# A list made later, three more up-products, and the first block of each group expert by expert

## The chip, the cores and the metric

The kernel runs on one core of a Trainium2 chip. The metric is device time in microseconds (us). The core has five engines that each run their own queue of instructions in order: TensorE (PE, with its weight loads shown apart as PEld), VectorE (DVE), ScalarE (ACT), GpSimd (POOL) and SyncE (SP, which here only issues DMA transfers). They wait for each other through semaphores.

## What is computed

The reference is one residual block of an encoder over 512 tokens of width 2048, in float32: a mixer (stick-breaking attention and forgetting attention, gated), then PEER, a retrieval of single-neuron experts, then a norm. The change touches PEER alone:

```python
q = (ht @ w_query).reshape(n_tok, 8, 2, 128)
scores = einsum('thpc,hpnc->thpn', q, sub_keys)
s1, i1 = top_k(scores[:, :, 0], 16); s2, i2 = top_k(scores[:, :, 1], 16)
cand_score = (s1[..., :, None] + s2[..., None, :]).reshape(n_tok, 8, 256)
cand_id = (i1[..., :, None] * 128 + i2[..., None, :]).reshape(n_tok, 8, 256)
top_score, pos = top_k(cand_score, 16)
expert_ids = take_along_axis(cand_id, pos); gates = softmax(top_score)
act = gelu(einsum('thkd,td->thk', expert_u[expert_ids], x))
out = einsum('thk,thkd->td', gates * act, expert_v[expert_ids])
```

So each token has 8 heads with 16 experts each, out of 16384.

## The kernel before, in words

The first 1300 us hold the mixer; then come the output projection, the second norm, and PEER. PEER treats its tokens in two ways.

**Dense tokens.** 352 tokens (`TD`) go through all experts. An "up-product" (`expert_up`, L532) makes the activations of 128 experts: it loads the weights in two halves (`wload`, L96), splits each into a high part `wh` (ACT, L108) and a low part `wl` (DVE, L109), and runs, per half, eight steps of three matmuls (L116 high by high, L117 high by low, L118 low by high), 48 matmuls in all into `psu`. There are 128 up-products. Raw weights `wr` have four buffers, `wh` and `wl` three each. Up-products made ahead (`early`, L618) store their result in device memory (`gact_sp`); `NS` of them, 54 before, are made that way: five behind each head's choice of experts for the dense tokens, and further ones between the gate tables.

The gates stand in 22 gate tables (L782 to L798), each for 16 tokens: PE products `psgt`, copied by ACT, sent to device memory (`gsp`) by POOL.

Then 16 groups of eight "weight tables" follow. `weigh(n)` (L813) takes the activations of 128 experts (`fetch`: loaded from `gact_sp`, L807, or made then by an up-product), for the first of a group loads the gates of the whole group into the one table buffer, which lies in the spare columns of h2 (three transfers on SP, L820, called `h<-gsp` in the profile), multiplies both on DVE (L822), and splits the result `wg` in high (ACT, L825) and low (DVE, L826). A group has eight blocks (`jb`), each with two outputs (`jj`), and each output sums over the group's eight expert tables `c`: 24 matmuls into `psy`. Behind an output, DVE adds it to `acc` (L846). The weights of output `jj` of a block are the `jj`-th half that its `wload` brings.

**Other tokens.** 128 tokens, and 32 more (the "second tile", `idx_b`, `gate_b`, `rstd_b`), take their experts' rows one by one: POOL gathers a row of 2048 numbers for each of 128 tokens (`row_of`, L554), DVE works on it for 2.35 us (L565, L574, L583, L594). These stand in a list `todo`; `pace` (L546) hands out a row behind splits of up-products and behind adds, at a rate that spreads them over the rest of the program. The list of the second tile (L746 to L763) is made by a product `psrep` of PE (L755) from DVE's `rep`, and copied out by DVE in four groups.

**What sets the order.** The code is written once; a layer below records the instructions and orders them with a list scheduler by its own costs, so an engine's queue isn't in the order of the code, but each engine runs its queue in order. `choose` (L650 to L711) is the choice of experts of one head, some 150 short DVE instructions.

Of the kernel before, what the change touches and what calls it, by code (L numbers as in the profile page):

```python
# [8 lines left out]
F32 = mybir.dt.float32  # L9
# [3 lines left out]
AF = mybir.ActivationFunctionType  # L13
ALU = mybir.AluOpType
# [4 lines left out]
P = 128  # L19
T = 512  # L20
NT = T // P
D = 2048
KC = D // P
HD = 128
NH = 8
NK = 128
TOPK = 16
HK = NH * TOPK
# [3 lines left out]
GC = 8  # L32
NG = NK // GC
JJ = D // (GC * P)
TB = 16
MB = 32
GB = P // MB
SB = HK // GB
TD = T - P - MB
# [1 line left out]
HT = NT - 2  # L41
CW = 112
UPS = 5
NS = NH * UPS + TD // TB - -(-(TD // TB) // 3)
SLOW = 0.8
LEAD = 1
NP = 4
# [3 lines left out]
def block_kernel(ctx, tc, xT, gains, w_vf, bf, w_qk, w_v, w_g, w_br, w_o, w_q, keysT, uT, vP, expert_u, expert_v, outT):  # L51
    nc = tc.nc
# [27 lines left out]
    ident = cp.tile([P, P], F32, name="ident")  # L80
    select(ident, zeros, 1, -1, ALU.not_equal, 1.0)
    g_sb = cp.tile([P, 3 * KC], F32, name="g_sb")
    nc.sync.dma_start(g_sb, gains)
    rstd = cp.tile([P, T], F32, name="rstd")
    rstd_t = cp.tile([P, NT], F32, name="rstd_t")
    one_c = ones[:, 0:1]

    acc = ap_.tile([P, KC, T], F32, name="acc")
# [6 lines left out]
    def wload(src, between=None, pace=None):  # L95

        out = []
        n = src.shape[-1] // 2
        for s in range(2):
            turn[0] += 1  # L100
            rp = more[0] if more and turn[0] % 2 else wp
            raw = rp.tile([P, WC], F32, tag="wr", name="wr", bufs=2)[:, :n]
            nc.sync.dma_start(raw, src[:, s * n:(s + 1) * n])
            if between and s == 0:
                between()
            hi = wp.tile([P, WC], F32R, tag="wh", bufs=3, name="wh")[:, :n]
            lo = wp.tile([P, WC], F32R, tag="wl", bufs=3, name="wl")[:, :n]
            nc.scalar.activation(hi, raw, AF.Copy)  # L108
            ins = nc.vector.tensor_tensor(lo, raw, hi.bitcast(F32), op=ALU.subtract)  # L109
            out.append((hi, lo))  # L110
            if pace:
                pace(ins, 0.5)
        return out

    def mm3(ps, wh, wl, ah, al, start, stop):
        nc.tensor.matmul(ps, wh, ah, start=start, stop=False)  # L116
        nc.tensor.matmul(ps, wh, al, start=False, stop=False)  # L117
        nc.tensor.matmul(ps, wl, ah, start=False, stop=stop)  # L118
# [19 lines left out]
    with ExitStack() as s1:  # L138
# [3 lines left out]
        with ExitStack() as s2:  # L142
# [21 lines left out]
            for k in range(KC):  # L164
# [3 lines left out]
                                               op1=ALU.subtract)  # L168
# [252 lines left out]
            ps = pa.tile([P, NT, NH], F32, tag="z1", name="psc")  # L421
# [5 lines left out]
            ps = pa.tile([P, T], F32, tag="z0", name="pscT")  # L427
# [34 lines left out]
        h2 = h2p.tile([P, KC, 2, T], F32R, name="h2")  # L462
        with ExitStack() as s2:
            op = pool("oproj", 1, cm=s2)
# [23 lines left out]
    gl = pool("gelu", 4)  # L488
# [129 lines left out]
    def early(n, pace=None):  # L618
        for _ in range(n):
            if len(started) < NS:  # L620
                c = len(started)
                nc.scalar.dma_start(gact_sp[c], expert_up(c, pace))
                started.append(c)

    with ExitStack() as s1:
# [88 lines left out]
        for h in range(NH):  # L714
            sc = []
            sv = se.tile([P, 2, HT, NK], F32, tag="sv", name="sv")
            for p in range(2):
                b = 2 * h + p
                if b == 1:
                    norm2()  # L720
                if b == 3:
                    token_rows(lambda k: acc[:, k, T - P:], h2g, accg)
                ps = pu.tile([P, T], F32, tag="pu", name="psq2")
                proj(ps, wload(w_q[b]), h2)
                q = se.tile([P, T], F32, tag="ab1", name="q2")
                nc.scalar.activation(q, ps, AF.Copy)
                kt = se.tile([P, NK], F32, tag="kt", name="kt")
                nc.sync.dma_start(kt, keysT[b])
                ps = psx.tile([P, NT, NK], F32, tag="psx", name="pss")
                for t in range(NT):  # L730
                    nc.tensor.matmul(ps[:, t], q[:, t * P:(t + 1) * P], kt, start=True, stop=True)
                nc.scalar.activation(sv[:, p], ps[:, :HT], AF.Copy)
                sc.append(ps[:, HT:])
            nc.scalar.dma_start(scores[h], sv)
            choose(h, sc, HT, NT - HT)


        for k in range(KC):
            tmp = gl.tile([P, TD], F32, tag="gl", name="h2n")
            nc.vector.scalar_tensor_tensor(tmp, acc[:, k, :TD], g_sb[:, KC + k:KC + k + 1], rstd[:, :TD], op0=ALU.mult,  # L740
                                           op1=ALU.mult)
            nc.scalar.activation(h2[:, k, 0, :TD], tmp, AF.Copy)
            nc.vector.tensor_tensor(h2[:, k, 1, :TD], tmp, h2[:, k, 0, :TD].bitcast(F32), op=ALU.subtract)


        nc.vector.scalar_tensor_tensor(idx, ia[:, NT - 1], float(NK), ib[:, NT - 1], op0=ALU.mult, op1=ALU.add)  # L746
        nc.vector.tensor_copy(ggate, gt[:, NT - 1])
        rep = se.tile([P, 2 * HK + 2], F32, tag="ab1", name="rep")
        nc.vector.scalar_tensor_tensor(rep[:, :HK], ia[:, NT - 2], float(NK), ib[:, NT - 2], op0=ALU.mult, op1=ALU.add)
        nc.vector.tensor_copy(rep[:, HK:2 * HK], gt[:, NT - 2])  # L750
        nc.vector.tensor_copy(rep[:, 2 * HK:], rstd_t[:, NT - 2:NT - 1].to_broadcast([P, 2]))
        spread = se.tile([P, GB, MB], F32, tag="kt", name="spread")
        nc.vector.tensor_copy(spread, ident[:, P - MB:].unsqueeze(1).to_broadcast([P, GB, MB]))
        ps = psx.tile([P, T], F32, tag="psx", name="psrep")
        nc.tensor.matmul(ps[:, :2 * HK + 2], spread.rearrange("p g m -> p (g m)"), rep, start=True, stop=True)  # L755
        for g in range(GB):
            rows = slice(g * MB, (g + 1) * MB)
            nc.vector.tensor_copy(idx_b[rows], ps[rows, g * SB:(g + 1) * SB])
            nc.vector.tensor_copy(ggate_b[rows], ps[rows, HK + g * SB:HK + (g + 1) * SB])
        nc.vector.tensor_copy(rstd_b, ps[:, 2 * HK:2 * HK + 1])  # L760
        nc.vector.tensor_copy(sel_b, ident[:, :MB])
        for g in range(1, GB):
            nc.vector.tensor_tensor(sel_b, sel_b, ident[:, g * MB:(g + 1) * MB], op=ALU.add)  # L763


        for h in range(NH):
            sv = se.tile([P, 2, HT, NK], F32, tag="sv", name="svl")
            nc.sync.dma_start(sv, scores[h])
            choose(h, [sv[:, p] for p in range(2)], 0, HT)
            early(UPS, pace)  # L770

        tr = []
        for n, src in enumerate((ia, ib, gt)):
# [8 lines left out]
        for tb in range(TD // TB):  # L782
            st = se.tile([P, NK, TB], F32, tag="st", name="st")
            for t4 in range(0, TB, 4):
                tk = slice(tb * TB + t4, tb * TB + t4 + 4)
                ab = [se.tile([P, 4, NK], F32, tag=f"ab{i}", bufs=2, name="ab") for i in range(2)]
                nc.vector.tensor_tensor(ab[1], i128.unsqueeze(1).to_broadcast([P, 4, NK]),
                                        tr[1][:, tk].unsqueeze(2).to_broadcast([P, 4, NK]), op=ALU.is_equal)
                ps = pg.tile([P, 4, NK], F32, tag="pg", name="psgt")
                for i in range(4):  # L790
                    t = tb * TB + t4 + i
                    nc.vector.tensor_scalar(ab[0][:, i], i128, tr[0][:, t:t + 1], tr[2][:, t:t + 1], op0=ALU.is_equal,  # L792
                                            op1=ALU.mult)
                    nc.tensor.matmul(ps[:, i], ab[0][:, i], ab[1][:, i], start=True, stop=True)
                nc.scalar.activation(st[:, :, t4:t4 + 4].rearrange("p n t -> p t n"), ps, AF.Copy)
            nc.gpsimd.dma_start(gsp[:, tb], st)
            if tb % 3:
                early(1, pace)  # L798

    ex = pool("exp", 1)  # L800
    extra.append(ex)
# [27 lines left out]
    ws = [weigh(0)]  # L829
# [3 lines left out]
    for grp in range(NG):  # L833
        while len(ws) < GC:
            ws.append(weigh(grp * GC + len(ws)))
        for jb in range(KC // JJ):
            w = wload(vP[grp, jb])
            for jj in range(JJ):
                j = jb * JJ + jj
                ps = (py, py2)[j % 2].tile([P, T], F32, tag="py", name="psy")  # L840
                for c in range(GC):
                    b = jj * GC + c
                    wh, wl = w[b // 8]
                    cc = slice(b % 8 * P, (b % 8 + 1) * P)
                    mm3(ps[:, :TD], wh[:, cc], wl[:, cc], ws[c][:, 0], ws[c][:, 1], c == 0, c == GC - 1)
                add = nc.vector.tensor_tensor(acc[:, j, :TD], acc[:, j, :TD], ps[:, :TD], op=ALU.add)  # L846
                pace(add, 1.0 / JJ)
        ws = []
# [83 lines left out]
```

## Time and profile before

| | |
|---|---|
| runs shown (3) | 3780.73 us median, 3780.49 to 3784.08 |
| profiled execution | 3777.61 us |
| its span in the trace | 3775.9 us |
| PE busy | 97% of the span |
| PEld busy | 90% |
| DVE busy | 69% |
| ACT busy | 34% |
| POOL busy | 14% |
| mean granted PE clock | 0.988 of full |

The profile is of one execution. Busy shares are means over stages that differ; what a stage waits for is read from the waits and the timeline of that stage. In a timeline, a row has the start, the duration, the engine, the line of the kernel, and output and inputs by name; in square brackets stands the time for which the engine was idle just before, and what released it. Matmuls overlap, so their pitch is read from the starts of two neighbours. Two levels of PE's clock occur: 2.4 GHz, where a matmul of 352 columns follows the one before after 0.16 us, and 1.2 GHz, where it takes 0.29 us.

### The profile page before, as it was taken

The numbers are of one execution on the slowest core, as the hardware profiler recorded it, in microseconds if no ns is written. First come the engines' busy times: TensorE is split into PE (matmuls) and PEld (weight loads), VectorE is DVE, ScalarE is ACT, GpSimd is POOL, SyncE is SP. The second block draws the span as 40 slices with busy tenths as digits, with TensorE's granted clock in tenths as the row PEclk, the third lists the DMA queues.
The fourth block names the chain that finished last, engine by engine and source line by source line (L and its number), as shares of the span: only waits on it lengthen the run. The fifth ranks groups of instructions, "written<-read, shape, count | busy, mean of one in ns | idle before, by whom it ended". The sixth has DMA issues, their size and how long they took to land.

```text
span 3775.9 us, 52068 instructions
## 1 busy us (share of the span) xinstructions
PE 3670.2 (97%) x20745; PEld 3381.2 (90%) x20745; DVE 2597.2 (69%) x3971; ACT 1290.8 (34%) x1824; POOL 530.6 (14%) x432
## 2 busy tenths in 40 slices
PE   9999999999999999899999898999999999999997
PEld 7888888888887878699999898999999999999997
DVE  5333445444555446899589888888789888988785
ACT  4334222232223223355356432333333333333333
POOL 0000000000000000011001122222223322322320
PEclk9999999999999999999999999999999999999999
DMA  4222222222224232377767899999889889989883
GB/s 142 79 78 77 98 95 95 87 90 81 88 95 138 95 101 97 106 267 275 274 245 274 290 340 326 353 342 331 318 334 372 327 334 337 366 330 343 327 306 110
DMA packets 233700, 827.25 MB, mean 219 GB/s; under 512 B 21736, under 2 KB 82664, under 8 KB 189680
## 3 DMA queue, kind: packets, MB, share of 16 engines
q1 hardware_dynamic: 174032, 450.30, 34.4%
q0 software_dynamic: 49920, 360.74, 24.9%
q10 hardware_dynamic: 9504, 12.88, 0.9%
q8 instruction: 163, 2.67, 0.3%
q14 instruction: 81, 0.66, 0.1%
HBM read 784.72 MB, written 39.11 MB: 218 GB/s over the span
## 4 chain that ended last, share of the span: by engine, by line
PE 83%; DVE 9%; DMA 4%; issue 2%; ACT 1%; SPq 0%; POOL 0%; DVEq 0%; POOLq 0%; ACTq 0%
PE psy L118 7%; PE psy L117 7%; PE psu L118 7%; PE psu L116 7%; PE psu L117 7%; PE psy L116 7%; PE psg L118 3%; PE psg L117 3%; PE psg L116 3%; PE psq L117 3%; PE psq L118 3%; PE psq L116 3%; DVE wl L109 2%; DVE ab L792 2%; PE psk L118 2%
## 5 line engine op out<-in xcount | busy, mean ns | idle before, releaser
L108 ACT ACTIVATE wh<-wr 128x1024 fp32r<-128x1024 f32 x768 | 813.8, 1060 | 1948.6 <-PE psy L117 583.1
L109 DVE TENSOR_TENSOR wl<-wr,wh 128x1024 fp32r<-128x1024 f32 x768 | 936.3, 1221 | 588.7 <-ACT wh L108 586.7
L116 PE MATMUL psy<-wg,wh 128*128 128x352 f32 x2048 | 667.5, 326 | 29.5 <-ACT wg L825 28.7
L117 PE MATMUL psy<-wg,wh 128*128 128x352 f32 x2048 | 670.5, 328 | 8.6 <-DVE wg L826 8.6
L118 PE MATMUL psu<-h,wl 128*128 128x352 f32 x2048 | 665.3, 325 | 12.8 <-DVE wl L109 12.7
L118 PE MATMUL psy<-wg,wl 128*128 128x352 f32 x2048 | 668.8, 328 | 7.4 <-DVE wl L109 7.2
L116 PE MATMUL psu<-h,wh 128*128 128x352 f32 x2048 | 666.5, 325 | 0.0
L117 PE MATMUL psu<-h,wh 128*128 128x352 f32 x2048 | 662.3, 323 | 0.0
L116 PEld LDWEIGHTS psy<-wg,wh 128*128 128x128 f32 x2048 | 389.8, 190 | 31.8 <-ACT wg L825 30.3
L117 PEld LDWEIGHTS psy<-wg,wh 128*128 128x128 f32 x2048 | 390.4, 191 | 10.5 <-DVE wg L826 10.4
L118 PEld LDWEIGHTS psu<-h,wl 128*128 128x128 f32 x2048 | 385.0, 188 | 16.3 <-DVE wl L109 16.3
L118 PEld LDWEIGHTS psy<-wg,wl 128*128 128x128 f32 x2048 | 389.7, 190 | 10.2 <-DVE wl L109 10.0
L117 PEld LDWEIGHTS psu<-h,wh 128*128 128x128 f32 x2048 | 386.2, 189 | 0.0
L116 PEld LDWEIGHTS psu<-h,wh 128*128 128x128 f32 x2048 | 385.9, 188 | 0.0
L558 POOL DMA_INDIRECT row<-eu,idx x128 | 180.8, 1413 | 903.0 <-DVE row L565 585.3
L583 DVE SCALAR_TENSOR_TENSOR acc<-row,gact,acc 128x2048 f32<-128x2048 f32 x128 | 300.2, 2346 | 9.3 <-DMA row<-ev,idx 9.2
L565 DVE SCALAR_TENSOR_TENSOR row<-row,rstd_t,h2g 128x2048 f32<-128x2048 f32 x128 | 300.3, 2346 | 0.0
L558 POOL DMA_INDIRECT row<-ev,idx x128 | 201.6, 1575 | 493.2 <-DVE acc L583 443.6
L116 PE MATMUL psq<-h,wh 128*128 128x512 f32 x512 | 205.2, 401 | 8.4 <-ACT wh L108 8.4
L117 PE MATMUL psq<-h,wh 128*128 128x512 f32 x512 | 206.1, 402 | 0.3 <-DVE h L167 0.3
L118 PE MATMUL psq<-h,wl 128*128 128x512 f32 x512 | 205.3, 401 | 0.1
L118 PE MATMUL psg<-h,wl 128*128 128x512 f32 x512 | 203.8, 398 | 0.0
(313 smaller groups left out, 5481.1 us busy)
## 6 DMA issues: line engine op xcount, KB each, us to landing
wr<-uT SPq DMA_DIRECT2D x256, 512.0 KB, 6.1
wr<-vP SPq DMA_DIRECT2D x256, 512.0 KB, 7.3
wr<-w_qk SPq DMA_DIRECT2D x64, 512.0 KB, 3.5
wr<-w_g SPq DMA_DIRECT2D x64, 512.0 KB, 3.5
gsp<-st POOLq DMA_DIRECT2D x22, 1024.0 KB, 4.5
wr<-w_br SPq DMA_DIRECT2D x32, 512.0 KB, 3.1
wr<-w_o SPq DMA_DIRECT2D x32, 512.0 KB, 3.2
wr<-w_q SPq DMA_DIRECT2D x32, 512.0 KB, 3.7
```

Of the source, the lines that this page charges most:

```text
L108: nc.scalar.activation(hi, raw, AF.Copy)
L109: ins = nc.vector.tensor_tensor(lo, raw, hi.bitcast(F32), op=ALU.subtract)
L116: nc.tensor.matmul(ps, wh, ah, start=start, stop=False)
L117: nc.tensor.matmul(ps, wh, al, start=False, stop=False)
L118: nc.tensor.matmul(ps, wl, ah, start=False, stop=stop)
L558: nc.gpsimd.indirect_dma_start(out=row.rearrange("p k q -> p (k q)"), out_offset=None, in_=table, in_offset=bass.IndirectOffsetOnAxis(ap=i ...
L565: nc.vector.scalar_tensor_tensor(row, row, rstd_t[:, NT - 1:NT], h2g, op0=ALU.mult, op1=ALU.mult, accum_out=gact[:, i:i + 1])
L583: nc.vector.scalar_tensor_tensor(accg, row, gact[:, i:i + 1], accg, op0=ALU.mult, op1=ALU.add)
L792: nc.vector.tensor_scalar(ab[0][:, i], i128, tr[0][:, t:t + 1], tr[2][:, t:t + 1], op0=ALU.is_equal, op1=ALU.mult)
```

## The change

It has three parts. The lines in the changed kernel lie one to ten further down.

First, the loop that normalises h2 for the dense tokens (`h2n`) is written ahead of the last head's `choose`, and the list of the second tile is wrapped in a function that is called behind the first five up-products.

```diff
+            if h == NH - 1:
+                for k in range(KC):
+                    tmp = gl.tile([P, TD], F32, tag="gl", name="h2n")
...
             choose(h, sc, HT, NT - HT)
-        for k in range(KC):
-            tmp = gl.tile([P, TD], F32, tag="gl", name="h2n")
...
+        def second_list():
...
             early(UPS, pace)
+            if h == 0:
+                second_list()
```

On PE the list's product (`psrep`) moves. Before, it stood among the first up-product's matmuls (`psu_11806`; the high parts of the next one, `psu_11870`, stand just ahead):

```order
L116 MATMUL psu_11806<-h2_8494,wh_11815 128x352
L117 MATMUL psu_11806<-h2_8494,wh_11815 128x352
L116 MATMUL psu_11870<-h2_8494,wh_11873 128x352
L117 MATMUL psu_11870<-h2_8494,wh_11873 128x352
L755 MATMUL psrep_11701<-rep_11695,spread_11699 128x258
L118 MATMUL psu_11806<-h2_8494,wl_11816 128x352
```

Now it stands at the end of the fifth up-product (`psu_12050`), ahead of the sixth:

```order
L117 MATMUL psu_12050<-h2_8494,wh_12059 128x352
L118 MATMUL psu_12050<-h2_8494,wh_12059 128x352
L119 MATMUL psu_12050<-h2_8494,wl_12060 128x352
L759 MATMUL psrep_12123<-rep_12117,spread_12121 128x258
L117 MATMUL psu_12228<-h2_8494,wh_12231 128x352
```

The product moved behind all 240 matmuls of five up-products; before, 28 stood ahead of it.

Second, three more up-products are made ahead, behind the gate tables.

```diff
+MORE = 3
-NS = NH * UPS + TD // TB - -(-(TD // TB) // 3)
+NS = NH * UPS + TD // TB - -(-(TD // TB) // 3) + MORE
...
             if tb % 3:
                 early(1, pace)
+        early(MORE, pace)
```

On SP, this is what stood at the end of the gate tables before: the weights of the first two blocks (`wr<-vP`), the loads of stored activations (`gl<-gact_sp`), and the last part of the first table load (`h2<-gsp`):

```order
L103 DMA wr_17364<-vP 128x1024
L103 DMA wr_17428<-vP 128x1024
L807 DMA gl_17235<-gact_sp_9651 128x352
L807 DMA gl_17237<-gact_sp_9651 128x352
L807 DMA gl_17249<-gact_sp_9651 128x352
L103 DMA wr_17434<-vP 128x1024
L807 DMA gl_17255<-gact_sp_9651 128x352
L103 DMA wr_17495<-vP 128x1024
L820 DMA h2_8494<-gsp_9623 128x6x128
L807 DMA gl_17261<-gact_sp_9651 128x352
```

And this is what stands there now, behind the six weight loads of the three up-products:

```order
L104 DMA wr_17489<-vP 128x1024
L104 DMA wr_17495<-vP 128x1024
L828 DMA h2_8494<-gsp_9623 128x6x128
L104 DMA wr_17559<-vP 128x1024
L104 DMA wr_17565<-vP 128x1024
L104 DMA wr_17626<-vP 128x1024
L104 DMA wr_17632<-vP 128x1024
L815 DMA gl_17433<-gact_sp_9651 128x352
L815 DMA gl_17435<-gact_sp_9651 128x352
L815 DMA gl_17447<-gact_sp_9651 128x352
```

The table's last part moved to behind the first two weight halves; the first three activations moved from behind the fifth half of the weights to behind the sixth.

Third, the first block of each group runs expert by expert: both outputs' sums are open at once, and for each expert table the three matmuls of output 0 and of output 1 follow each other; the two adds stand behind both.

```diff
         for jb in range(KC // JJ):
             w = wload(vP[grp, jb])
+            pss = [(py, py2)[jj % 2].tile([P, T], F32, tag="py", name="psy") for jj in range(JJ)]
+            order = [(jj, c) for c in range(GC) for jj in range(JJ)]
+            for jj, c in (order if jb == 0 else sorted(order)):
+                b = jj * GC + c
+                wh, wl = w[b // 8]
+                cc = slice(b % 8 * P, (b % 8 + 1) * P)
+                mm3(pss[jj][:, :TD], wh[:, cc], wl[:, cc], ws[c][:, 0], ws[c][:, 1], c == 0, c == GC - 1)
             for jj in range(JJ):
                 j = jb * JJ + jj
-                ps = (py, py2)[j % 2].tile([P, T], F32, tag="py", name="psy")
-                for c in range(GC):
...
+                ps = pss[jj]
                 add = nc.vector.tensor_tensor(acc[:, j, :TD], acc[:, j, :TD], ps[:, :TD], op=ALU.add)
                 pace(add, 1.0 / JJ)
```

On DVE, the start of group 10 before: the splits of the first block's second half and of the second block's halves (`wl`), the multiply of the next group's first table (L822), the adds (L846), a gathered row (L583):

```order
L109 TENSOR_TENSOR wl_25618<-wr_25615,wh_25617 128x1024
L109 TENSOR_TENSOR wl_25679<-wr_25676,wh_25678 128x1024
L822 TENSOR_TENSOR gl_25603<-gl_25603,h2_8494 128x352
L846 TENSOR_TENSOR acc_79<-acc_79,psy_25621 128x352
L583 SCALAR_TENSOR_TENSOR acc_79<-row_25647,gact_9641,acc_79 128x16x128
L109 TENSOR_TENSOR wl_25685<-wr_25682,wh_25684 128x1024
L846 TENSOR_TENSOR acc_79<-acc_79,psy_25650 128x352
L826 TENSOR_TENSOR wg_26227<-gl_25603,wg_26227 128x352
```

And now (the low part of the next group's table is L834, the adds L856, the row L584):

```order
L110 TENSOR_TENSOR wl_25624<-wr_25621,wh_25623 128x1024
L110 TENSOR_TENSOR wl_25688<-wr_25685,wh_25687 128x1024
L830 TENSOR_TENSOR gl_25609<-gl_25609,h2_8494 128x352
L834 TENSOR_TENSOR wg_26233<-gl_25609,wg_26233 128x352
L856 TENSOR_TENSOR acc_79<-acc_79,psy_25627 128x352
L584 SCALAR_TENSOR_TENSOR acc_79<-row_25678,gact_9641,acc_79 128x16x128
L856 TENSOR_TENSOR acc_79<-acc_79,psy_25628 128x352
L584 SCALAR_TENSOR_TENSOR acc_79<-row_25682,gact_9641,acc_79 128x16x128
L110 TENSOR_TENSOR wl_25694<-wr_25691,wh_25693 128x1024
```

Between the multiply and the split of the second block's second half (`wl_25685` before, `wl_25694` now) stood one add and one row; now there stand a low part, two adds and two rows.

## Rows read from the trace of the kernel before

**Rows 1.** Busy time of engines: us, share of the span, instructions.
```profile
PE 3670.2 (97%) x20745; PEld 3381.2 (90%) x20745; DVE 2597.2 (69%) x3971; ACT 1290.8 (34%) x1824; POOL 530.6 (14%) x432
```

**Rows 2.** Waits of PE, 1500 to 3776 us: total, times, longest.
```profile
PE psy L116 <- ACT wg L825: 28.7, 6, 14.3
...
PE psrep L755 <- DVE rep L749: 11.2, 1, 11.2
PE psy L117 <- DVE wg L826: 8.6, 4, 5.1
```

**Rows 3.** Timeline of PE at the list: start, us, then the instruction.
```profile
1595.53 1.20 PE L755 MATMUL psrep<-rep,spread 128*128 128x258 f32 x2 [11.21 <-DVE rep L749]
1601.98 0.66 PE L118 MATMUL psu<-h,wl 128*128 128x352 f32 x1 [5.25 <-DVE wl L109]
```

**Rows 4.** Stretches, busy us (instructions): PE, PEld, DVE, ACT, POOL; clock, DMA.
```profile
1650.00:1700.00 50.00, 48.39 (x302) 48.10 (x301) 50.00 (x174) 27.79 (x49) 7.61 (x5) 1.00 0.75 273
1800.00:1850.00 50.00, 50.00 (x313) 50.00 (x312) 28.79 (x25) 15.90 (x19) 5.64 (x6) 1.00 0.77 267
```

**Rows 5.** Timeline of PE at the end of the gate tables.
```profile
2113.22 1.17 PE L794 MATMUL psgt<-ab 128*128 128x128 f32 x8 [0.46 <-DVE ab L792]
2128.71 0.96 PE L116 MATMUL psy<-wg,wh 128*128 128x352 f32 x2 [14.33 <-ACT wg L825]
```

**Rows 6.** Timeline of DVE at the same place.
```profile
2127.60 1.40 DVE L822 TENSOR_TENSOR gl<-gl,h 128x352 f32<-128x352 f32 x3 [12.63 <-DMA h<-gsp]
```

**Rows 7.** Timeline of PE, group 10: its first matmul, its only wait.
```profile
3065.04 0.32 PE L116 MATMUL psy<-wg,wh 128*128 128x352 f32 x1
...
3078.69 0.43 PE L118 MATMUL psy<-wg,wl 128*128 128x352 f32 x1 [1.50 <-DVE wl L109]
```

**Rows 8.** DVE's busy us (instructions) at the list; clock, DMA.
```profile
1568.40:1600.70 32.30, 32.25 (x145) 0.78 0.20 70
```

**Rows 9.** DVE by lines, 1590 to 1602 us: busy us, mean ns.
```profile
L758 DVE CAST idx_b<-psrep 32x32 uint32<-32x32 f32 x4 | 0.7, 182 | 0.0
```

**Rows 10.** Stored activations as a tile, 2105 to 2145 us, twelve loads.
```profile
DMA to landing us min/median/max: 2.3/5.8/6.2
```

**Rows 11.** Timeline of DVE, group 10.
```profile
3060.69 0.53 DVE L826 TENSOR_TENSOR wg<-gl,wg 128x352 fp32r<-128x352 f32 x1 [0.57 <-ACT wg L825]
...
3066.17 1.23 DVE L109 TENSOR_TENSOR wl<-wr,wh 128x1024 fp32r<-128x1024 f32 x1 [2.62 <-ACT wh L108]
3074.28 0.53 DVE L822 TENSOR_TENSOR gl<-gl,h 128x352 f32<-128x352 f32 x1 [6.88 <-DMA h<-gsp]
3074.72 0.52 DVE L846 TENSOR_TENSOR acc<-acc,psy 128x352 f32<-128x352 f32 x1
3075.16 2.35 DVE L583 SCALAR_TENSOR_TENSOR acc<-row,gact,acc 128x2048 f32<-128x2048 f32 x1
3077.42 1.22 DVE L109 TENSOR_TENSOR wl<-wr,wh 128x1024 fp32r<-128x1024 f32 x1
```

**Rows 12.** Timeline of PE at the starts of groups 4 and 6.
```profile
2411.09 0.43 PE L116 MATMUL psy<-wg,wh 128*128 128x352 f32 x1 [3.05 <-ACT wg L825]
...
2579.86 0.56 PE L118 MATMUL psy<-wg,wl 128*128 128x352 f32 x1 [2.13 <-DVE wl L109]
2580.22 0.49 PE L116 MATMUL psy<-wg,wh 128*128 128x352 f32 x1
2580.51 0.49 PE L117 MATMUL psy<-wg,wh 128*128 128x352 f32 x1
```

**Rows 13.** Waits of all engines, 2590 to 3750 us: total, times, longest.
```profile
DVE gl L822 <- DMA h<-gsp: 51.5, 8, 7.4
...
DVE acc L583 <- DMA row<-ev,idx: 9.2, 13, 1.8
...
PE psy L118 <- DVE wl L109: 5.0, 5, 1.8
```

More of the change, by code (lines that the diff above doesn't have):

```diff
@@ L734, in block_kernel @@
             nc.scalar.dma_start(scores[h], sv)
-            choose(h, sc, HT, NT - HT)
-        for k in range(KC):
-            tmp = gl.tile([P, TD], F32, tag="gl", name="h2n")
[L740 to L743, printed above, removed]
+            if h == NH - 1:
+                for k in range(KC):
+                    tmp = gl.tile([P, TD], F32, tag="gl", name="h2n")
+                    nc.vector.scalar_tensor_tensor(tmp, acc[:, k, :TD], g_sb[:, KC + k:KC + k + 1], rstd[:, :TD], op0=ALU.mult,
+                                                   op1=ALU.mult)
+                    nc.scalar.activation(h2[:, k, 0, :TD], tmp, AF.Copy)
+                    nc.vector.tensor_tensor(h2[:, k, 1, :TD], tmp, h2[:, k, 0, :TD].bitcast(F32), op=ALU.subtract)
@@ L746, in block_kernel @@
+            choose(h, sc, HT, NT - HT)
         nc.vector.scalar_tensor_tensor(idx, ia[:, NT - 1], float(NK), ib[:, NT - 1], op0=ALU.mult, op1=ALU.add)
         nc.vector.tensor_copy(ggate, gt[:, NT - 1])
[L748 to L763, printed above, removed]
+        def second_list():
+            rep = se.tile([P, 2 * HK + 2], F32, tag="ab1", name="rep")
+            nc.vector.scalar_tensor_tensor(rep[:, :HK], ia[:, NT - 2], float(NK), ib[:, NT - 2], op0=ALU.mult, op1=ALU.add)
+            nc.vector.tensor_copy(rep[:, HK:2 * HK], gt[:, NT - 2])
+            nc.vector.tensor_copy(rep[:, 2 * HK:], rstd_t[:, NT - 2:NT - 1].to_broadcast([P, 2]))
+            spread = se.tile([P, GB, MB], F32, tag="kt", name="spread")
+            nc.vector.tensor_copy(spread, ident[:, P - MB:].unsqueeze(1).to_broadcast([P, GB, MB]))
+            ps = psx.tile([P, T], F32, tag="psx", name="psrep")
+            nc.tensor.matmul(ps[:, :2 * HK + 2], spread.rearrange("p g m -> p (g m)"), rep, start=True, stop=True)
+            for g in range(GB):
+                rows = slice(g * MB, (g + 1) * MB)
+                nc.vector.tensor_copy(idx_b[rows], ps[rows, g * SB:(g + 1) * SB])
+                nc.vector.tensor_copy(ggate_b[rows], ps[rows, HK + g * SB:HK + (g + 1) * SB])
+            nc.vector.tensor_copy(rstd_b, ps[:, 2 * HK:2 * HK + 1])
+            nc.vector.tensor_copy(sel_b, ident[:, :MB])
+            for g in range(1, GB):
+                nc.vector.tensor_tensor(sel_b, sel_b, ident[:, g * MB:(g + 1) * MB], op=ALU.add)
@@ L837, in block_kernel @@
             w = wload(vP[grp, jb])
+            pss = [(py, py2)[jj % 2].tile([P, T], F32, tag="py", name="psy") for jj in range(JJ)]
[5 more added lines that the diff above has]
+                mm3(pss[jj][:, :TD], wh[:, cc], wl[:, cc], ws[c][:, 0], ws[c][:, 1], c == 0, c == GC - 1)
             for jj in range(JJ):
                 j = jb * JJ + jj
-                ps = (py, py2)[j % 2].tile([P, T], F32, tag="py", name="psy")
-                for c in range(GC):
[L842 to L845, printed above, removed]
+                ps = pss[jj]
                 add = nc.vector.tensor_tensor(acc[:, j, :TD], acc[:, j, :TD], ps[:, :TD], op=ALU.add)
```

## The prediction

> **What bounds the kernel now.** I began with the page's first part: TensorE (PE) is busy for 97% of the span, VectorE (DVE) for 69% [rows 1]. On average PE is the bound, and a change can only win idle time of PE. The waits of PE from 1500 us on say where that is [rows 2]: 28.7 us in six waits for the high part of a weight table (`wg`), 11.2 us in one wait at the list of the second tile, 8.6 us for low parts of `wg`. The change goes at all three. So I read three places in order of time, first on PE, then on the engine or queue that releases it: the list (near 1600 us), the end of the gate tables (near 2120 us), and the start of a group, for which group 10 stands.
>
> At the list PE waits 11.21 us for DVE's `rep`, and right behind it 5.25 us more for `wl`, the low part of the first up-product's second half [rows 3]. DVE is what ends both waits, and afterwards it stays full: in the 50 us from 1650 it is busy for 50.00 us, PE for 48.39 [rows 4]. At the end of the gate tables PE idles for 14.33 us [rows 5], because DVE waits 12.63 us for the gate table [rows 6]. In group 10 PE waits only 1.50 us, for the split of the second block's second half [rows 7].
>
> **Part (a), the list behind the first five up-products, h2's loop ahead of the last choose.** Nothing is removed. In PE's order 240 matmuls of up-products stand ahead of the product `psrep`, where 28 stood, so the 11.21 us wait for `rep` goes. What is late next is the `wl` that PE waits for today: its split lies on DVE behind the whole last choose, before and after. In the 32.30 us up to that split DVE is busy for 32.25 [rows 8], so it comes sooner only by the work that leaves this stretch, and by the order that is the list's own short operations: four casts of `idx_b` with 0.7 us [rows 9], four copies of the same size beside them, and a few more, by their sizes about as much again: 2 us. The rest of PE's idle time only moves from `rep` to `wl`. The list work comes later, where DVE is full [rows 4]. I take **−2 us**; bounds −11 (the whole wait goes) and +1 (the list work comes back where PE waits for DVE).
>
> **Part (b), three more up-products behind the last gate table.** They aren't extra work, since 128 are made in any case; the change puts 3 × 48 = 144 matmuls into the idle stretch. At 50.00 / 313 = 0.16 us each [rows 4] they take 23.0 us, from about 2113.1 (where the last gate-table products would end without their waits, [rows 5]) to 2136.1. If the wait stayed whole, the first down matmul would come at 2128.7 + 23.0 = 2151.7, since these 23.0 us leave a later place. By SP's order the third part of the table load now stands ahead of the second block's weights, but the loads of stored activations stand behind the weights' sixth half. Its buffer comes free when the second half is split, and that split writes a buffer that the last up-product's first half holds until 2113.1 + 120 × 0.16 = 2132.3. With the split's two parts (DVE's takes 1.2 us by [rows 11], ACT's is put at the same), the loads go out at about 2134.9. They land after 5.8 us by the median of twelve, 2.3 to 6.2 [rows 10]. From the first multiply to the first matmul it is 1.1 us (2127.60 to 2128.71, [rows 5, 6]). So PE starts at 2134.9 + 5.8 + 1.1 = 2141.8, 9.9 us sooner than 2151.7. About one goes to the fifth expert's load, which waits for one of four buffers. I take **−9 us**; bounds −14 (landing in 2.3) and −5 (the second set of loads at 6.2 as well).
>
> **Part (c), the first block expert by expert, groups 0 to 6.** Each expert's weights get 6 matmuls of cover (0.96 us) where they had 3. The cost: both outputs of the block finish together at its end. Before, the first finished 24 matmuls (3.84 us) sooner, and its add to `acc`, with the gathered row behind it, lay beside the second output's matmuls. Now two adds and up to two gathered rows stand on DVE ahead of the split of the second block's second half. With T the group's first matmul, the first output ends at about T + 45 × 0.16 + 0.3 = T + 7.5; then an add 0.44, a row 2.26, an add 0.44, a row 2.26, a split 1.22 (pitches and length from [rows 11]), together T + 14.1. PE needs that split at T + 12.15 (3078.69 − 1.50 − 3065.04, [rows 7]). So where two rows stand there 1.95 us are lost, by DVE's order in groups 0, 3 and 6: **+5.9**. With one row it is T + 11.9, nothing. For the waits at the starts of groups 1 to 6 I take **0**; bounds −4 (half of the 8.6 us for low parts, [rows 2]) and +4 (a start wait of group 6, which now follows a group of stored products only; nearest row 3.05, [rows 12]).
>
> **Part (d), groups 7 to 14.** There DVE's multiply for the next group stands in the same place, and waits for that group's table load: 51.5 us in 8 waits, 6.44 each [rows 13]. Before, PE lost little by it, because behind it came one add, one row and the split. Now there come the next group's low part, both adds and one or two rows. The split ahead of the multiply starts at T + 1.13 and ends at T + 2.36 [rows 7, 11]; the mean wait puts the multiply at T + 8.8 (in group 10 T + 9.24). The low part starts 1.1 later (0.53 of multiply, 0.57 of waiting for ACT's high part), then 0.44 for it, 0.44 + 2.26 + 0.44 for add, row, add, and 1.22 for the split, 5.9 in all [rows 11]: T + 14.7 with one row, T + 16.96 with two. Against T + 12.15 that is 2.55 and 4.81 us. By the order four of these groups have one row (7, 9, 11, 13) and four two: 4 × 2.55 + 4 × 4.81 = 29.4. Five waits of 5.0 us in sum stand there today [rows 13], so **+24.4**. Bounds: +2.8 (rival 1) and +32 (each load as late as the longest wait, 7.4, less the 6.44, eight times).
>
> **The clock.** Of six waits of over 2 us around the starts of groups, five were followed by matmuls 0.29 us apart, the lower level, 1.2 GHz; the smallest of them is the one of 2.13 us, with 11 such matmuls behind it. The wait of 3.05 us was not followed by any [rows 12], nor that of 1.50 [rows 7]. Eleven matmuls cost 11 × (0.29 − 0.16) = 1.43 us. For the eight stalls of (d), 8 × 5/6 × 1.43 = **+9.5 us**; bounds 0 and, with every stall of (c) and (d), +16.
>
> The Trainium skill ("TensorE: Matmul & The Clock Gate", section "HAM oscillation — how this bites in real kernels") says that a loop whose waits let the clock fall pays the slow restart anew in every turn. By that rule all eight restarts count, 11.4 us and not 9.5, and the time would be 1.9 us longer; the trace agrees in five cases and disagrees in the one at 2411.09.
>
> **Sum.** −2 − 9 + 5.9 + 24.4 + 9.5 = +28.8. The profiled execution took 3777.61 us (span 3775.9), so 3806.4; the median of the runs shown lies 3.1 above it: **3810**.
>
> **Rivals.** (1) The other side, no slower: the third part of the table load lands before about T + 6, so the multiply never holds the adds. For it: the load is issued behind a weight load whose buffer an earlier split frees, and another DVE order may free it sooner. Against it: SP's order around these loads is the same, and it has to land 2.7 us sooner. Then only the two-row groups lose 1.95, four of them here, too little for the clock to fall by the 1.50 case: −2 − 9 + 5.9 + (7.8 − 5.0) = −2.3, giving 3778. It decides at T + 6. (2) The stall is not made up. DVE's work for a half with a row is 0.44 + 2.26 + 1.14 (the split's pitch) = 3.84 us, PE's 24 × 0.16 = 3.84, so after a stall there is no slack, and the waits for gathered rows (9.2 us in 13, [rows 13]) reach PE: +9, 3819. Against it: not every half has a row. (3) The list edit gives all it could: 11.2 + 5.25 less the 2 that I count, 14.5 more, 3795. Against it stands the full DVE of [rows 4, 8].
>
> **How the numbers follow.** Forecast 0.60, rival 1 0.16, rival 2 0.17, rival 3 0.07. A measurement of this kernel tells 0.2% (7.6 us) from no change, so "same" is 3773 to 3788. Faster comes from the lower third of rival 1 and from (a) and (b) both at their best: 0.09. Same: the rest of rival 1 and the forecast with (d) at half: 0.13. Slower: 0.78. The forecast's own range, with its bounds, is 3792 to 3828; with the rivals, 3778 to 3832.
>
> **What would show it.** PE's wait for `rep` gone and one of about 14 us for `wl` in its place; the first down matmul near 2140; in groups 7 to 14 waits of PE for `wl` of 2 to 5 us, each behind a DVE multiply that waits for the table, with matmuls 0.29 us apart behind them. Wrong would be: no such waits in groups 8, 10, 12, 14, or the multiply at T + 6.

## The result, and the profile after

The changed kernel takes 3806.6 us (median of four runs, 3799.4 to 3807.4) against 3782.1 for the kernel before, measured beside it: a ratio of 1.0064, 95% interval 1.0052 to 1.0077. It is slower by 24.5 us. The forecast was 3810, on the side that came.

The profiled execution, the fastest of the four, took 3799.35 us, with a span of 3797.7 where the one before had 3775.9, so the profiles account for 21.8 us. Its page begins so:

```profile
PE 3684.2 (97%) x20745; PEld 3391.3 (89%) x20745; DVE 2599.3 (68%) x3971; ACT 1285.9 (34%) x1822; POOL 516.8 (14%) x432
```

PE's share is the same as in [rows 1]. The averages tell nothing of the change; the waits of PE from 1500 us on do (total, times, longest):

```profile
PE psy L119 <- DVE wl L110: 23.3, 11, 3.3
PE psu L119 <- DVE wl L110: 22.7, 12, 15.6
PE psy L117 <- ACT wg L833: 14.4, 6, 5.5
PE psy L118 <- DVE wg L834: 12.9, 9, 3.9
```

Against [rows 2], the wait for the high parts of `wg` is halved (28.7 to 14.4), the one for its low parts has grown (8.6 to 12.9), the one for `rep` is gone, the one of up-products for `wl` holds one of 15.6 us now, and a new row stands first: down matmuls that wait 23.3 us for the low part of their weights, where they waited 7.2 in the kernel before. The first two places on PE's timeline, to be held against [rows 3, 5]:

```profile
1601.18 0.66 PE L119 MATMUL psu<-h,wl 128*128 128x352 f32 x1 [15.62 <-DVE wl L110]
...
2140.80 0.66 PE L117 MATMUL psy<-wg,wh 128*128 128x352 f32 x1 [5.45 <-ACT wg L833]
```

At the list the same matmul starts 0.8 us sooner, after one wait in place of two. At the gate tables, the three up-products (23.0 us) have been run ahead of the first down matmul, which comes at 2140.80, 12.1 us later than before: 10.9 us won up to there, by the list and the up-products together.

Now the stretch from the first down matmul of group 7 to that of group 15, in which both kernels do the same work. Before (us; busy of PE, PEld, DVE, ACT, POOL with instructions; clock, DMA share, GB/s):

```profile
2691.61:3691.01 999.40, 993.10 (x6145) 989.84 (x6145) 825.09 (x717) 322.44 (x385) 285.27 (x179) 1.00 0.89 334
```

After:

```profile
2683.68:3713.00 1029.32, 1003.59 (x6146) 998.25 (x6145) 829.08 (x719) 321.52 (x385) 273.36 (x180) 0.99 0.88 325
```

The same 6145 matmuls take 29.9 us more, and the granted clock is lower. PE's idle time in the stretch rises from 6.1 to 25.7 us, by 19.6. Most of the other 10.3 us is the clock: by the starts of all matmuls, 91 follow the one before at some 0.29 us (1.2 GHz) instead of 0.16, where 22 did, which costs 9.0 us more. The span adds up by stretches: −10.9 up to the first down matmul, +3.0 in groups 0 to 6 (542.9 us against 562.9 less the 23.0 of work that left them), +29.9 in groups 7 to 14, −0.2 behind: +21.8.

Group 10 shows how. DVE after, to be held against [rows 11]:

```profile
3070.72 1.22 DVE L110 TENSOR_TENSOR wl<-wr,wh 128x1024 fp32r<-128x1024 f32 x1 [2.62 <-ACT wh L109]
3076.58 0.52 DVE L830 TENSOR_TENSOR gl<-gl,h 128x352 f32<-128x352 f32 x1 [4.63 <-DMA h<-gsp]
3077.67 0.53 DVE L834 TENSOR_TENSOR wg<-gl,wg 128x352 fp32r<-128x352 f32 x1 [0.56 <-ACT wg L833]
3078.11 0.51 DVE L856 TENSOR_TENSOR acc<-acc,psy 128x352 f32<-128x352 f32 x1
3078.54 2.35 DVE L584 SCALAR_TENSOR_TENSOR acc<-row,gact,acc 128x2048 f32<-128x2048 f32 x1
3080.80 0.51 DVE L856 TENSOR_TENSOR acc<-acc,psy 128x352 f32<-128x352 f32 x1
3081.24 2.34 DVE L584 SCALAR_TENSOR_TENSOR acc<-row,gact,acc 128x2048 f32<-128x2048 f32 x1
3083.50 1.22 DVE L110 TENSOR_TENSOR wl<-wr,wh 128x1024 fp32r<-128x1024 f32 x1
```

And PE there, against [rows 7]:

```profile
3069.59 0.32 PE L117 MATMUL psy<-wg,wh 128*128 128x352 f32 x1
...
3082.41 0.43 PE L117 MATMUL psy<-wg,wh 128*128 128x352 f32 x1 [0.33 <-ACT wh L109]
...
3084.77 0.43 PE L119 MATMUL psy<-wg,wl 128*128 128x352 f32 x1 [1.77 <-DVE wl L110]
```

The multiply (L830) waits for the table load until T + 7.0, with T = 3069.59. Behind it come the low part, an add, a row, an add, a row, and only then the split that PE needs, whose end at T + 15.1 starts PE again. For all eight groups the waits of both engines are these:

```profile
DVE gl L830 <- DMA h<-gsp: 49.9, 8, 7.6
...
PE psy L119 <- DVE wl L110: 21.7, 8, 3.3
```

DVE's wait for the tables is what it was (51.5 in [rows 13]), but what PE waits for `wl` went from 5.0 to 21.7 us.

### The profile page after: what moved, and what is told of

Same layout as the page of the kernel before. It is cut to its first block, busy times and chain, and to the rows that moved or that the text cites. A ratio compares the mean times of both kernels' runs of the same rounds, so it can differ in the third digit from the quotient of the medians.

```text
span 3797.7 us, 52087 instructions
## 1 busy us (share of the span) xinstructions
PE 3684.2 (97%) x20745; PEld 3391.3 (89%) x20745; DVE 2599.3 (68%) x3971; ACT 1285.9 (34%) x1822; POOL 516.8 (14%) x432
## 4 chain that ended last, share of the span: by engine, by line
PE 80%; DVE 11%; DMA 3%; issue 3%; ACT 1%; POOL 0%; SPq 0%; DVEq 0%; POOLq 0%; ACTq 0%
PE psy L119 7%; PE psu L119 7%; PE psu L117 7%; PE psu L118 7%; PE psy L118 7%; PE psy L117 7%; PE psg L118 3%; PE psg L119 3%; PE psg L117 3%; PE psq L118 3%; PE psq L119 3%; PE psq L117 3%; DVE wl L110 2%; DVE ab L798 2%; DVE row L566 2%
## 5 line engine op out<-in xcount | busy, mean ns | idle before, releaser
L119 PE MATMUL psy<-wg,wl 128*128 128x352 f32 x2048 | 671.9, 330 | 23.4 <-DVE wl L110 23.3
L117 PE MATMUL psy<-wg,wh 128*128 128x352 f32 x2048 | 672.7, 329 | 18.0 <-ACT wg L833 14.4
L118 PE MATMUL psy<-wg,wh 128*128 128x352 f32 x2048 | 675.3, 330 | 13.0 <-DVE wg L834 12.9
L584 DVE SCALAR_TENSOR_TENSOR acc<-row,gact,acc 128x2048 f32<-128x2048 f32 x128 | 300.3, 2346 | 8.6 <-DMA row<-ev,idx 8.4
L856 DVE TENSOR_TENSOR acc<-acc,psy 128x352 f32<-128x352 f32 x256 | 132.4, 518 | 109.2 <-PE psy L119 108.4
```

Source lines behind the costliest of these rows:

```text
L584: nc.vector.scalar_tensor_tensor(accg, row, gact[:, i:i + 1], accg, op0=ALU.mult, op1=ALU.add)
```

## Experiments

All ratios are to the kernel before, run beside the experiment on the same chip (medians 3778.2, 3779.2 and 3779.5 us in the three sets), with 95% intervals.

**The three edits apart.** Theory: the loss is the third edit's, by way of the multiply that holds adds, rows and split; the first wins next to nothing, the second 9 us. First the list alone (`MORE = 0`, the block's loop as before):

> Only the first edit: h2's loop ahead of the last choose, the list of the second tile behind the first five up-products; no further up-products, outputs one after the other. Theory (DVE is what PE waits for near 1600 us, so the wait only changes its name): PE's waits for rep (11.2 us) and wl (5.25 us) become one of some 15.6 us for wl, and the time is 0 to 2 us under the kernel before, 3780 to 3782 against 3782. Rival (the wait was the list's): the wait goes, some 14 us less, 3768.

Measured: 3777.6, ratio 1.0001 (0.9991 to 1.0010). On PE one wait stands for two, as long as expected:

```profile
1599.26 0.66 PE L119 MATMUL psu<-h,wl 128*128 128x352 f32 x1 [15.62 <-DVE wl L110]
```

The wait was DVE's and not the list's; rival 3 falls. Then the up-products alone (the second part of the change on the kernel before):

> Only the second edit: three more up-products behind the last gate table. Theory (they fill most of PE's 14.33 us of idle time there): the first down matmul comes 10 to 11 us sooner than 2128.7 + 23.0 = 2151.7, and the time is about 9 us under the kernel before, 3773 against 3782. Rival (they only push the wait on, or the start of group 6, which now follows stored products, gives it back): within 3 us of the kernel before, 3779 to 3785.

Measured: 3773.2, ratio 0.9985 (0.9976 to 0.9993), 5.7 us won where 9 were expected. The first down matmul came at 2140.31, 11.4 us sooner than 2151.7, but the stretch from there to group 7 took 546.7 us against 562.9 − 23.0 = 539.9: 6.8 us went back there, into waits at the starts of groups and lower clock behind them. Between theory and rival, then: the place is right, and part of the win is given back. Then the block's order alone (the third part of the change on the kernel before):

> Only the third edit: the first block of each group expert by expert. Theory (adds and rows held behind the multiply that waits for the table load, then the lower clock): 25 to 38 us over the kernel before, 3807 to 3820, with PE's waits for wl of 2 to 5 us in groups 7 to 14. Rival (the loss comes from the three edits together, by the number of rows that fall there): within 8 us of the kernel before, 3774 to 3790.

Measured: 3802.0, ratio 1.0064 (1.0051 to 1.0077): 24 us slower by itself, just under the 25 to 38 that were expected. The stretch of groups 7 to 14 took 1032.0 us, against 999.4 before. And the first two without the third:

> The first two edits without the third. Theory (the edits add up): some 10 us under the kernel before, 3772 against 3782, and 34 under the changed kernel. Rival (the loss sits in the first two edits, for example in the start of group 6 or in the stored activations): 3790 or more.

Measured: 3772.5, ratio 0.9978 (0.9970 to 0.9987), 8 us faster than before. The first two add up within their intervals (1.0001 and 0.9985 alone). With the third they do not quite: 0.9978 and 1.0064 would make 1.0042, and the whole change was measured, in another set of runs, at 1.0064. But the third alone loses as much as the whole change, and without it nothing is lost.

**Where the third edit loses.** The whole change, with a limit on the groups:

```diff
-            for jj, c in (order if jb == 0 else sorted(order)):
+            for jj, c in (order if jb == 0 and grp <= 6 else sorted(order)):
```

> The whole change, but expert by expert only in groups 0 to 6; from group 7 on one output after the other. Theory (the loss sits in groups 7 to 14): the loss goes, 0 to 5 us over the kernel with the first two edits alone (8 us under the kernel before), so 3 to 8 us under the kernel before. Rival (an equal loss in every first block that runs so): 7 of 16 groups remain, some 14 us of the 32, so 5 us or more over the kernel before.

Measured: 3772.9, ratio 0.9985 (0.9974 to 0.9995), groups 7 to 14 in 998.9 us. The loss sits in the groups whose next table load DVE waits for, and not in every block that runs expert by expert.

**The multiply moved.** The whole change, but the multiply that waits is issued behind the add of the second block's first output:

```diff
+        late = hold.get(n // GC - 1) if n % GC == 0 and n >= 8 * GC else None
+        with ExitStack() as held:
+            if late:
+                held.enter_context(tc.issue_after(late))
+            nc.vector.tensor_tensor(...)     # the multiply by the table
...
+                if jb == 1 and jj == 0:
+                    hold[grp] = add.ins
```

> The whole change, but in groups 7 to 14 the multiply that waits for the next group's table load is issued behind the add of the second block's first output, so behind the late split; nothing else moves. Theory (the multiply holds adds, rows and split): PE's waits for wl of 1.8 to 3.3 us in these groups fall to 0 in groups with one row and to 2 us at most with two (the split ends at T + 11.9 or T + 14.1 against T + 12.15), and the time is 20 to 30 us under the changed kernel, 0 to 6 us under the kernel before. Rival (the order of experts itself costs, on PE or in the two open sums): the time stays within 6 us of the changed kernel, 24 over the kernel before.

Measured: 3768.7, ratio 0.9972 (0.9962 to 0.9983). It is faster than both kernels, with PE still going expert by expert. DVE in group 10 (T = 3055.84):

```profile
3063.34 0.52 DVE L861 TENSOR_TENSOR acc<-acc,psy 128x352 f32<-128x352 f32 x1 [5.14 <-PE psy L119]
3063.78 2.35 DVE L584 SCALAR_TENSOR_TENSOR acc<-row,gact,acc 128x2048 f32<-128x2048 f32 x1
3066.04 0.51 DVE L861 TENSOR_TENSOR acc<-acc,psy 128x352 f32<-128x352 f32 x1
3066.47 2.35 DVE L584 SCALAR_TENSOR_TENSOR acc<-row,gact,acc 128x2048 f32<-128x2048 f32 x1
3068.74 1.22 DVE L110 TENSOR_TENSOR wl<-wr,wh 128x1024 fp32r<-128x1024 f32 x1
```

The first add now starts at T + 7.5, when PE has finished the output, and the split ends at T + 14.1, both as worked out in part (c). PE waits some 0.33 and 0.75 us in the four groups with two rows and not at all in the others, and DVE no longer waits for a table load. PE's wait for `wl` in groups 7 to 14, against 21.7 us in the whole change:

```profile
PE psy L119 <- DVE wl L110: 3.0, 4, 0.8
```

That shows the mechanism: PE still goes expert by expert, and nearly all of its wait went with the wait that stood ahead of the adds. What is left comes from the two rows themselves; whether the order is then free is measured below.

**The rows moved.** The whole change with the multiply where it was, and the rows of a first block handed out behind the second block's adds:

```diff
-                pace(add, 1.0 / JJ)
+                if jb:
+                    pace(add, (2.0 if jb == 1 else 1.0) / JJ)
```

> The whole change, but the gathered rows that follow a first block's adds are handed out behind the second block's adds instead; the multiply stays where it is. Theory (multiply and rows together): without rows the split ends at 3.6 us behind the multiply, T + 12.4 by the mean and T + 13.5 where the load lands at T + 9.9, so waits of 0 to 1.4 us are left, and the time is 18 to 30 us under the changed kernel. Rival (the load's wait alone is what PE feels): within 6 us of the changed kernel.

Measured: 3818.1, ratio 1.0098 (1.0083 to 1.0114): slower still, and neither theory nor rival had that. The trace tells why. At the split the waits are 0 to 1.02 us, as expected, but later on DVE in group 10 the rows now stand in a bunch:

```profile
3102.18 2.34 DVE L584 SCALAR_TENSOR_TENSOR acc<-row,gact,acc 128x2048 f32<-128x2048 f32 x1
3104.45 0.51 DVE L856 TENSOR_TENSOR acc<-acc,psy 128x352 f32<-128x352 f32 x1
3104.88 2.34 DVE L584 SCALAR_TENSOR_TENSOR acc<-row,gact,acc 128x2048 f32<-128x2048 f32 x1
3107.14 0.51 DVE L856 TENSOR_TENSOR acc<-acc,psy 128x352 f32<-128x352 f32 x1
3109.71 2.35 DVE L584 SCALAR_TENSOR_TENSOR acc<-row,gact,acc 128x2048 f32<-128x2048 f32 x1 [2.06 <-DMA row<-ev,idx]
```

The third of these rows waits 2.06 us for its gather, a fourth stands behind it, and then PE waits:

```profile
3115.94 0.66 PE L119 MATMUL psy<-wg,wl 128*128 128x352 f32 x1 [4.40 <-DVE wl L110]
```

Five such waits in groups 7 to 14 make 23.4 us; and the groups up to 6 took 558.2 us, 15.3 more than in the whole change, 12.0 of it idle time of PE. This run could not tell the theories apart by its time. With both moves:

> The whole change with both moves: the multiply behind the second block's first add in groups 7 to 14, and the rows of a first block handed out one block later. Theory: no wait for wl at the third and fourth half in any group from 7 on; the time is that of the first two edits alone, 8 us under the kernel before, within 4 us. Rival (the rows that are now bunched behind the second block make a wait of their own): over the kernel with the multiply moved alone.

Measured: 3799.6, ratio 1.0061 (1.0047 to 1.0075). The rival had it: the rows moved by one block cost some 31 us over the kernel with the multiply moved alone. Most of that is the bunch, since the same rows spread evenly cost 8 (below). So the rows were moved again, without a bunch:

```diff
-                pace(add, 1.0 / JJ)
+                if jb:
+                    pace(add, 8 / 7 / JJ)
```

> The whole change, but the gathered rows are handed out behind the adds of blocks 1 to 7 alone, at 8/7 of the rate, so none falls between a first block's adds and the next splits, and none is bunched. The multiply stays where it is. Theory (multiply and rows together make the loss): waits of 0 to 1 us at the fourth half in groups 7 to 14, 3 to 8 us in sum instead of 25.7, groups 7 to 14 within 5 us of the 999 us of before, and the time 0 to 8 us under the kernel before. Rival (the wait for the load is enough by itself, rows or not): some 24 us over the kernel before.

Measured: 3782.7, ratio 1.0013 (1.0004 to 1.0022). With the multiply still ahead of the adds, groups 7 to 14 take 1000.7 us, against 999.4 before and 1029.3 with the whole change. DVE waits for the tables as long as ever there, PE for `wl` hardly:

```profile
DVE gl L830 <- DMA h<-gsp: 51.4, 8, 7.5
...
PE psy L119 <- DVE wl L110: 4.3, 5, 1.0
```

So the wait for the load costs PE much only with the rows behind it: both halves of the mechanism are shown. The time missed the expected 0 to 8 us under the kernel before at another place: from the first down matmul to group 7 it takes 554.4 us, 11.5 more than the whole change does, with these waits of PE (12.9 and 14.4 us in the whole change):

```profile
PE psy L118 <- DVE wg L834: 23.1, 10, 6.2
PE psy L117 <- ACT wg L833: 19.4, 7, 5.9
```

**What the moved multiply is worth.** In turn (the block's loop as before), with the multiply behind the second block's first add:

> The first two edits, outputs one after the other, and in groups 7 to 14 the multiply behind the second block's first add. It tells whether expert by expert wins anything in the kernel with the multiply moved (10 us under the kernel before). Theory (it wins only some waits at the starts of groups 1 to 6): 7 to 10 us under the kernel before, at most 3 us over that kernel. Rival (expert by expert is worth more): 4 us or more over it.

Measured: 3763.6, ratio 0.9964 (0.9951 to 0.9977), the lowest of all: further under the kernel before than the 7 to 10 us that were expected, and 0.8 per mille under the same with expert by expert, which the intervals don't tell apart. PE waits in groups 7 to 14 (to 3670 us) for this alone:

```profile
PE psu L119 <- DVE wl L110: 0.2, 1, 0.2
```

The kernel before lost 6.1 us to such waits in groups 7 to 14 itself. The stretch of these groups with the multiply moved, expert by expert and then in turn:

```profile
2681.96:3680.72 998.76, 993.99 (x6146) 989.51 (x6145) 828.05 (x719) 322.86 (x385) 277.05 (x180) 1.00 0.90 335
2683.20:3673.05 989.85, 989.63 (x6147) 988.56 (x6145) 831.10 (x719) 324.19 (x385) 279.42 (x180) 1.00 0.91 338
```

In these two executions expert by expert takes 8.9 us more in groups 7 to 14, with 4.8 us of idle time of PE against 0.2, and 2.6 less in groups 0 to 6 (540.3 against 542.9). So it won nothing that was measured, and in groups 7 to 14 it was not free. Two further steps from the kernel with the multiply moved, rows spread and six up-products, won nothing:

> The whole change with the multiply moved and the rows handed out behind the adds of blocks 1 to 7 at 8/7 of the rate. Theory: the waits of 0.34 + 0.75 us that were left in groups with two rows go, and those of 1.1 us in groups 0, 3 and 6: some 4 to 8 us under the kernel with the multiply moved alone, so 14 to 18 under the kernel before. Rival (a denser hand-out leaves DVE no slack in blocks 1 to 7): over that kernel.

Measured: 3776.6, ratio 0.9993 (0.9984 to 1.0002). Groups 7 to 14 fell to 993.4 us (998.8 with the multiply moved alone), but the groups up to 6 rose from 540.3 to 551.8, where PE waits 30.8 us for parts of `wg` instead of 20.4. So the time is over that kernel's, as the rival had it. What delays `wg` there wasn't traced.

> The whole change with the multiply moved, and six more up-products behind the last gate table instead of three. Theory (what is left of PE's wait there, 5.4 us, comes from loads of stored activations that stand behind weights whose buffers the last up-product frees, however many there are): the wait stays at 4 to 6 us, and the time within 4 us of the kernel with three and the multiply moved. Rival (more cover hides the rest): the wait goes, 5 to 8 us under it.

Measured: 3777.0, ratio 0.9997 (0.9989 to 1.0006). The wait at the first down matmul stays, as expected:

```profile
2162.37 0.66 PE L117 MATMUL psy<-wg,wh 128*128 128x352 f32 x1 [4.61 <-ACT wg L838]
```

But the time is some 8 us (by the medians) to 9 us (by the ratios) over that with three up-products. Up to group 7 it took 526.2 us, where 540.3 − 23.0 = 517.3 would have been no loss. These groups lose 8.9 us; why they cost more with more products stored wasn't tried.

## Why the prediction was right, step by step

The sum was +28.8, and +24.5 was measured (+21.8 between the two profiled executions). By stretches of the profiles: −10.9 where (a) and (b) had −11, +3.0 in groups 0 to 6 where (c) had +5.9, +29.9 in groups 7 to 14 where (d) and the clock had +33.9. The mechanism was right; two of its terms were too large.

**(a) The list, −2.** Right in kind: one wait of 15.62 us for `wl` where I said about 14. Alone it is worth nothing that its interval shows (1.0001, 0.9991 to 1.0010).

**(b) The up-products, −9.** Right in place and nearly in time: the stored loads went out at 2134.07 (worked out: 2134.9), the first multiply started at 2139.69 and the first matmul at 2140.80 (2141.8). The net win was smaller, 5.7 us, since the groups up to 6 gave 6.8 back. In the prediction that stood only as the upper bound of (c), +4 for group 6.

**(c) Groups 0 to 6, +5.9.** Half of it came: in groups 0, 3 and 6 PE's waits behind the two rows are 0.6 to 1.1 us in sum each, 2.8 in all, not 3 × 1.95; the four matmuls told under (d) stand ahead of the wait here too. Whether the cover at the starts is worth something isn't shown: with the third edit alone these groups took 560.3 us against 562.9 before, but with the list edit alone they took 560.4.

**(d) Groups 7 to 14, +24.4.** Right in place and cause, too large by 5: idle time of PE rose by 19.6 us, and the waits for `wl` are 21.7 us where 29.4 was worked out. By kind of group it came out the other way round, so the sum is as near as it is partly by luck. With one row (7, 9, 11, 13) the waits for `wl` are 3.0 to 3.3 us, for 2.55 worked out, since the multiply comes at T + 9.2 to 10.0; with two they are 1.8 to 2.8, for 4.81. There the load lands sooner (T + 7.0 to 8.8), and PE's queue has four matmuls of the next block's two sums ahead of the one that waits, a place in the order that I had not read as far as that (group 10 of the changed kernel; `wl_25694` is what PE waits for). In the groups with one row they do not stand there: 74 matmuls of the group precede the wait, against 78.

```
L118 MATMUL psy_25698<-wg_25113,wh_25693 128x352
L117 MATMUL psy_25764<-wg_25113,wh_25754 128x352
L118 MATMUL psy_25764<-wg_25113,wh_25754 128x352
L117 MATMUL psy_25765<-wg_25113,wh_25760 128x352
L118 MATMUL psy_25765<-wg_25113,wh_25760 128x352
L119 MATMUL psy_25698<-wg_25113,wl_25694 128x352
```

**The clock, +9.5.** Matmuls at the lower level cost 9.0 us more in groups 7 to 14: five of the eight stalls were followed by them, 10 to 18 each. The reading behind the price was not complete. Behind its first down matmul, the kernel before has seven waits of over 2 us at the starts of groups, not six, and the smallest is 2.11 us, in group 5, with 11 such matmuls behind it. A wait of 1.79 us in group 14 was followed by 11 too (both from the kernel before):

```profile
2477.25 0.43 PE L117 MATMUL psy<-wg,wh 128*128 128x352 f32 x1 [2.11 <-DVE wg L826]
...
3579.45 0.43 PE L118 MATMUL psy<-wg,wl 128*128 128x352 f32 x1 [1.79 <-DVE wl L109]
```

So 1.95 us, in rival 1, could not be taken as too little for the clock to fall.

**The rivals.** Rival 1 (the load lands before T + 6) fell: the loads landed from T + 7.0 on. Rival 2 (the stall isn't made up) shows only where rows are bunched, in the runs with them moved by one block. Rival 3 fell with the first experiment.

## What to carry to other kernels

An engine that runs its queue in order hands every wait on to what stands behind it. So a change of order on PE is priced on the queue of the engine that feeds it: find the one instruction there that waits for a transfer, and add up what must now pass behind it before PE's next operand. If that sum is the loss, moving the waiting instruction behind the operand is the cheaper edit: here it took the changed kernel from 24 us above the kernel before to 10 below it. The rest of that engine's work has to stay spread out, though: with the gathered rows bunched behind the next block, nearly all of the win was gone again (1.0061).

## What was not expected of the hardware

How long a wait was does not settle whether the clock fell behind it. In group 7 PE waited 3.29 us, and the matmuls behind it kept the pitch of 0.16 us:

```profile
2699.13 0.43 PE L119 MATMUL psy<-wg,wl 128*128 128x352 f32 x1 [3.29 <-DVE wl L110]
2699.40 0.32 PE L117 MATMUL psy<-wg,wh 128*128 128x352 f32 x1
2699.56 0.32 PE L118 MATMUL psy<-wg,wh 128*128 128x352 f32 x1
```

In group 8 it waited 1.84 us, and soon behind it 11 matmuls came 0.29 us apart (1.2 GHz):

```profile
2826.45 0.43 PE L119 MATMUL psy<-wg,wl 128*128 128x352 f32 x1 [1.84 <-DVE wl L110]
...
2827.05 0.49 PE L119 MATMUL psy<-wg,wl 128*128 128x352 f32 x1
2827.34 0.49 PE L117 MATMUL psy<-wg,wh 128*128 128x352 f32 x1
```

In all, five of the eight stalls were followed by 10 to 18 such matmuls, and three by none. What decides it stays open.
